# A projection with bias and residual: bias spread by a VectorE shuffle, wider dummy products, early casts on two engines, last store in two column pieces

## Chip, cores, metric

One core of a Trainium2 chip (trn2). The metric is the device time of one execution in microseconds (us). The profile's "span", from its first to its last recorded instruction, is about 1.8 us shorter. Names: PE is TensorE, PEld its weight loads, DVE VectorE, ACT ScalarE, POOL GpSimd, SP SyncE; a "q" behind a name is that engine's instruction queue.

## The reference

```python
batch, m, k, n = 16, 512, 1024, 768          # all fp32
out = np.matmul(x, weight) + bias + residual
```

The 8192 rows are handled as 64 tiles of 128 rows, in eight blocks of eight.

## The kernel before

Per tile: ACT casts x to bf16, PE transposes it (four transposes of paired bf16 words), DVE copies the transposed tile out of PSUM, PE makes 16 products, and DVE adds the result to the residual, to which POOL has already added the bias. The first three tiles go through their products weight quarter by weight quarter, since the weights arrive in quarters. All big loads and stores stand in one list and go through the queue of SP:

```python
HEAD_ORDER = [('bias',), ('warm', 10), ('cast', 0, 'v'), ('cast', 1, 's'), ('tr', 0), ('tr', 1),
 ('wc', 0, 0, 's'), ('wc', 0, 1, 'v'), ('warm', 4), ('mm', 0, 0), ('mm', 1, 0),
 ('cast', 2, 'v'), ('cast', 3, 's'), ('tr', 2), ('tr', 3), ('wc', 1, 0, 's'), ('wc', 1, 1, 'v'),
 # ... cut: the other quarters
 ('cast', 4, 's'), ('mm', 0, 3), ('mm', 1, 3), ('mm', 2, 3)]
ORDER = [('x', 0, 0, 2), ('w', 0, 0, 2), ('x', 0, 2, 4), ('w', 1, 0, 2), ('w', 2, 0, 2), ('w', 3, 0, 2),
 ('x', 0, 4, 6), ('x', 0, 6, 8), ('r', 0, 0, 5), ('x', 1, 0, 4), ('r', 0, 5, 8), ('r', 1, 0, 5),
 ('x', 1, 4, 8), ('x', 2, 0, 8), ('r', 1, 5, 8), ('r', 2, 0, 8), ('x', 3, 0, 8), ('s', 0, 0, 8),
 # ... cut: x, r (residual) and s (store) of the later blocks
 ('s', 4, 0, 8), ('s', 5, 0, 8), ('s', 6, 0, 8), ('s', 7, 0, 5), ('s', 7, 5, 7), ('s', 7, 7, 8)]
```

An entry is (kind, block, first tile, end tile). `'v'` and `'s'` name DVE and ACT, `('warm', n)` is n dummy products that keep PE busy. The bias is one row; a product with a row of ones spreads it over the partitions:

```python
    K_(nc.scalar.dma_start(out=bias_row, in_=bias[None, :]))       # first instruction of ACT's queue
    # ... cut: memsets
    make_identity(nc, ident)
    for _ in range(WARM):                                           # 10
        K_(nc.tensor.matmul(PO[0][:, 0:256], lhsT=warm[:, 0:P], rhs=warm, start=True, stop=True))

    def bias_rows():
        bias_ps = PO[HEAD - 1]
        for n0, nl in chunks:                                       # 512 and 256 columns
            K_(nc.tensor.matmul(bias_ps[:, n0:n0 + nl], lhsT=ones_row,
                                rhs=bias_row[:, n0:n0 + nl], start=True, stop=True))
        K_(nc.vector.tensor_copy(out=bias_sb, in_=bias_ps))
```

The program fixes the order of each engine's instructions (`K_` keeps it), and an instruction that waits holds up the work behind it: below, the cast of tile 0 on DVE stands behind a waiting instruction for 6.2 us.

Of the kernel before, what the change touches and what calls it, by code (L numbers as in the profile page):

```python
# [9 lines left out]
FP32 = mybir.dt.float32  # L10
BF16 = mybir.dt.bfloat16
P = 128
J = 8
X_SLOTS = 2
RO_SLOTS = 4
HEAD = 3
XT_N = 4
XB_N = 4
WARM = 10
EARLY_END = 6  # L20
TMP_SLOT = {0: 3}
ADDS = [6, 0, 7, 8, 1, 9, 2, 10, 3, 11, 4, 12, 5, 13, 14, 15]
HEAD_ORDER = [('bias',), ('warm', 10), ('cast', 0, 'v'), ('cast', 1, 's'), ('tr', 0), ('tr', 1),
 ('wc', 0, 0, 's'), ('wc', 0, 1, 'v'), ('warm', 4), ('mm', 0, 0), ('mm', 1, 0),
 ('cast', 2, 'v'), ('cast', 3, 's'), ('tr', 2), ('tr', 3), ('wc', 1, 0, 's'), ('wc', 1, 1, 'v'),
 ('mm', 2, 0), ('mm', 0, 1), ('mm', 1, 1), ('mm', 2, 1), ('wc', 2, 0, 's'), ('wc', 2, 1, 'v'),
 ('mm', 0, 2), ('mm', 1, 2), ('mm', 2, 2), ('wc', 3, 0, 's'), ('wc', 3, 1, 'v'),
 ('cast', 4, 's'), ('mm', 0, 3), ('mm', 1, 3), ('mm', 2, 3)]
ORDER = [('x', 0, 0, 2), ('w', 0, 0, 2), ('x', 0, 2, 4), ('w', 1, 0, 2), ('w', 2, 0, 2), ('w', 3, 0, 2),
 ('x', 0, 4, 6), ('x', 0, 6, 8), ('r', 0, 0, 5), ('x', 1, 0, 4), ('r', 0, 5, 8), ('r', 1, 0, 5),  # L30
 ('x', 1, 4, 8), ('x', 2, 0, 8), ('r', 1, 5, 8), ('r', 2, 0, 8), ('x', 3, 0, 8), ('s', 0, 0, 8),
 ('r', 3, 0, 8), ('x', 4, 0, 8), ('r', 4, 0, 8), ('s', 1, 0, 8), ('x', 5, 0, 8), ('r', 5, 0, 8),
 ('s', 2, 0, 8), ('x', 6, 0, 8), ('r', 6, 0, 8), ('s', 3, 0, 8), ('x', 7, 0, 8), ('r', 7, 0, 8),
 ('s', 4, 0, 8), ('s', 5, 0, 8), ('s', 6, 0, 8), ('s', 7, 0, 5), ('s', 7, 5, 7),
 ('s', 7, 7, 8)]


@with_exitstack
def kernel(
# [8 lines left out]
    nc = tc.nc  # L48
# [4 lines left out]
    N = weight.shape[1]  # L53
    n_q = K // (2 * P)
    n_t = M // P
    n_s = n_t // J
    chunks = [(0, 512), (512, N - 512)]

    x_d = x2d.rearrange("(S p j) k -> S p j k", p=P, j=J)
    res_d = res2d.rearrange("(S p j) n -> S p j n", p=P, j=J)  # L60
    out_d = out2d.rearrange("(S p j) n -> S p j n", p=P, j=J)
    w_d = weight.rearrange("(q p e) n -> p q e n", p=P, e=2)

    sb = ctx.enter_context(tc.tile_pool(name="sb", bufs=1))
    ps = ctx.enter_context(tc.tile_pool(name="ps", bufs=1, space=bass.MemoryType.PSUM))

    def fixed(pool, name, n, shape, dt):
        return [pool.tile(shape, dt, name=f"{name}", tag=f"{name}{i}", bufs=1) for i in range(n)]

    X = fixed(sb, "x_tile", X_SLOTS, [P, J, K], FP32)  # L70
    R = fixed(sb, "ro", RO_SLOTS, [P, J, N], FP32)
    XB = fixed(sb, "xb", XB_N, [P, K], BF16)
    XT = fixed(sb, "xt", XT_N, [P, n_q, P, 2], BF16)
    PO = fixed(ps, "psum_o", HEAD, [P, N], FP32)
    PT = fixed(ps, "pt", 2, [P, n_q, P], FP32)
    (w_sb,) = fixed(sb, "w_sb", 1, [P, n_q, 2, N], BF16)
    (bias_sb,) = fixed(sb, "bias_sb", 1, [P, N], FP32)
    (bias_row,) = fixed(sb, "bias_row", 1, [1, N], FP32)
    (ones_row,) = fixed(sb, "ones_row", 1, [1, P], FP32)
    (ident,) = fixed(sb, "ident", 1, [P, P], FP32)  # L80
    (warm,) = fixed(sb, "warm", 1, [P, 256], BF16)
    (warm_a,) = fixed(sb, "warm_a", 1, [1, 2], FP32)
    K_ = tc.keep_in_program_order
    w_st = R[1]

    done = set()
    queue = list(ORDER)

    def pump():
        while queue:  # L90
            kind, S, j0, j1 = queue[0]
            if kind == "w":
                need = []
            elif kind == "x":
                need = [("cast", J * (S - X_SLOTS) + j) for j in range(j0, j1)] if S >= X_SLOTS else []
            elif kind == "r":
                need = [("store", S - RO_SLOTS, j) for j in range(j0, j1)] if S >= RO_SLOTS else []
                if S == 1:
                    need = [("wcast", n_q - 1)]
                if S in TMP_SLOT.values():  # L100
                    need = [("add", t) for t in range(EARLY_END) if TMP_SLOT[t // J] == S]
            else:
                need = [("out", J * S + j) for j in range(j0, j1)]
            if not all(n in done for n in need):
                return
            queue.pop(0)
            if kind == "w":
                K_(nc.sync.dma_start(out=w_st[:, 2 * S + j0:2 * S + j1, :], in_=w_d[:, S, j0:j1, :]))
                continue
            if kind == "x":  # L110
                K_(nc.sync.dma_start(out=X[S % X_SLOTS][:, j0:j1, :], in_=x_d[S, :, j0:j1, :]))
            elif kind == "r":
                K_(nc.sync.dma_start(out=R[S % RO_SLOTS][:, j0:j1, :], in_=res_d[S, :, j0:j1, :]))
            else:
                K_(nc.sync.dma_start(out=out_d[S, :, j0:j1, :], in_=R[S % RO_SLOTS][:, j0:j1, :]))
                done.update(("store", S, j) for j in range(j0, j1))
            done.update((kind, J * S + j) for j in range(j0, j1))

    def mark(*what):
        done.add(what)  # L120
        pump()

    def cast(t, how="s"):
        if t < n_t:
            assert ("x", t) in done, t
            src, dst = X[t // J % X_SLOTS][:, t % J, :], XB[t % XB_N]
            if how == "sv":
                K_(nc.scalar.copy(out=dst[:, 0:K // 2], in_=src[:, 0:K // 2]))
                K_(nc.vector.tensor_copy(out=dst[:, K // 2:K], in_=src[:, K // 2:K]))
            else:  # L130
                K_((nc.scalar.copy if how == "s" else nc.vector.tensor_copy)(out=dst, in_=src))  # L131
            mark("cast", t)
# [12 lines left out]
    def mm(t, n0, nl, q, e):  # L145
        K_(nc.tensor.matmul(  # L146
            PO[t % HEAD][:, n0:n0 + nl], lhsT=XT[t % XT_N][:, q, :, e],
            rhs=w_sb[:, q, e, n0:n0 + nl],
            start=(q == 0 and e == 0), stop=(q == n_q - 1 and e == 1),
        ))  # L150

    def row(t, n0=0, nl=N):
        return R[t // J % RO_SLOTS][:, t % J, n0:n0 + nl]

    def tmp(t):
        return R[TMP_SLOT[t // J]][:, t % J, :]
# [17 lines left out]
    def finish(t):  # L174
        p = PO[t % HEAD]
        if t < EARLY_END:
            K_(nc.vector.tensor_add(out=tmp(t), in0=p, in1=bias_sb))  # L177
            mark("fin", t)
        else:
            assert ("add", t) in done, t  # L180
            K_(nc.vector.tensor_add(out=row(t), in0=p, in1=row(t)))  # L181
            mark("out", t)

    K_(nc.scalar.dma_start(out=bias_row, in_=bias[None, :]))
    K_(nc.vector.memset(warm, 0.0))  # L185
    K_(nc.vector.memset(ones_row, 1.0))
    K_(nc.vector.memset(warm_a, 0.0))
    K_(nc.scalar.copy(out=warm_a, in_=warm_a))  # L188
    make_identity(nc, ident)
    for _ in range(WARM):  # L190
        K_(nc.tensor.matmul(PO[0][:, 0:256], lhsT=warm[:, 0:P], rhs=warm, start=True, stop=True))  # L191

    def bias_rows():
        bias_ps = PO[HEAD - 1]
        for n0, nl in chunks:
            K_(nc.tensor.matmul(  # L196
                bias_ps[:, n0:n0 + nl], lhsT=ones_row, rhs=bias_row[:, n0:n0 + nl],
                start=True, stop=True,
            ))
        K_(nc.vector.tensor_copy(out=bias_sb, in_=bias_ps))  # L200

    pump()
    for kind, *a in HEAD_ORDER:
        if kind == "bias":
            bias_rows()
        elif kind == "cast":
            cast(*a)
        elif kind == "warm":
            for _ in range(a[0]):
                K_(nc.tensor.matmul(PO[1][:, 0:256], lhsT=warm[:, 0:P], rhs=warm, start=True, stop=True))  # L210
        elif kind == "tr":
            transp(a[0])
        elif kind == "wc":
            q, e, eng = a
            copy = {"v": nc.vector.tensor_copy, "s": nc.scalar.copy, "g": nc.gpsimd.tensor_copy}[eng]
            K_(copy(out=w_sb[:, q, e, :], in_=w_st[:, 2 * q + e, :]))  # L216
            if (q, e) == (n_q - 1, 1):
                mark("wcast", q)
        else:
            for e in range(2):  # L220
                for n0, nl in chunks:
                    mm(a[0], n0, nl, a[1], e)
    pump()
    for t in range(HEAD - 1):
        finish(t)
        pool_adds(t)

    for t in range(HEAD, n_t):
# [10 lines left out]
    t = n_t - 1  # L239
    tail = [(PO[t % HEAD], 0, 512), (PO[(t - 2) % HEAD], 512, N - 512)]  # L240
    for p, n0, nl in tail:
        for q in range(n_q):
            for e in range(2):
                K_(nc.tensor.matmul(  # L244
                    p[:, 0:nl], lhsT=XT[t % XT_N][:, q, :, e], rhs=w_sb[:, q, e, n0:n0 + nl],
                    start=(q == 0 and e == 0), stop=(q == n_q - 1 and e == 1),
                ))
        K_(nc.vector.tensor_add(out=row(t, n0, nl), in0=p[:, 0:nl], in1=row(t, n0, nl)))  # L248
    mark("out", t)
    pump()  # L250
    assert not queue, queue
# [30 lines left out]
```

## Time and profile before

| what | before | from |
|---|---|---|
| time | 211.45 us median | 4 runs, 211.37 to 211.54 |
| PE busy | 97% of the span | page, part 1 |
| DMA engines, SP's queue | 97.6% of their time | page, part 3 |
| one tile on PE in steady state | 3.036 us | chain in order of time |

These are lines of the page of the kernel before, from its parts 1, 2 and 3. In part 2 each digit is the busy share of one fortieth of the span, in tenths.

```profile
PE 204.3 (97%) x1308; PEld 133.6 (64%) x1308; DVE 104.7 (50%) x139; ACT 68.0 (32%) x68; POOL 114.6 (55%) x70
...
PE   7999999999999999999999999999999999999992
...
DMA  6999999999999999999999999999999999999785
...
q1 hardware_dynamic: 5184, 87.03, 97.6%
```

PE and the DMA engines are both full. PE alone is not the whole story: whatever makes PE earlier needs its data earlier from a queue that has hardly a gap.

The next lines are the timeline of the kernel before in its head. The columns are start, duration, engine, line, operation, what it writes and reads, count, and in brackets the idle time before it with what ended that.

```profile
3.30 2.92 PE L196 MATMUL psum_o<-bias_row,ones_row 1*128 1x512 f32 x4
5.53 1.04 ACT L131 CAST xb<-x_tile 128x1024 bf16<-128x1024 f32 x1 [2.78 <-DMA x_tile<-in_x_dram]
6.26 0.96 DVE L200 COPY bias_sb<-psum_o 128x768 f32<-128x768 f32 x1 [5.12 <-PE psum_o L196]
7.13 0.68 DVE L131 CAST xb<-x_tile 128x1024 bf16<-128x1024 f32 x1
8.26 1.91 PE L139 MATMUL pt<-ident,xb 128*128 128x128 f32 x8
10.82 2.11 PE L146 MATMUL psum_o<-w_sb,xt 128*128 128x512 bf16 x8
14.15 6.75 PE L146 MATMUL psum_o<-w_sb,xt 128*128 128x512 bf16 x40 [0.35 <-DVE xt L140]
```

The bias product starts at 3.30 with no wait for a load, so the bias landed by then. The first x piece lands at 5.53 (ACT's cast), but DVE first copies the bias and casts tile 0 only at 7.13. PE ends its head with 40 products from 14.15 to 20.90.

What the loads leave in slack is read from ACT's casts of tiles 8 to 11 and 12 to 15, in the timeline of ACT alone:

```profile
31.32 3.89 ACT L131 CAST xb<-x_tile 128x1024 bf16<-128x1024 f32 x4 [8.74 <-DMA x_tile<-in_x_dram]
43.61 3.89 ACT L131 CAST xb<-x_tile 128x1024 bf16<-128x1024 f32 x4 [8.41 <-DMA x_tile<-in_x_dram]
```

and from PE's transposes of tiles 8 and 12, in the timeline of PE around 33 and 45 us:

```profile
32.88 0.60 PE L139 MATMUL pt<-ident,xb 128*128 128x128 f32 x4
...
45.03 0.60 PE L139 MATMUL pt<-ident,xb 128*128 128x128 f32 x4
```

Tile 8's cast ends at 31.32 + 1.04 = 32.36, 0.52 us before PE's transpose (0.41 before its first weight load); tile 12's ends at 44.65, 0.38 us before (0.27). A PE more than that ahead would have to wait there.

### The profile page before, as it was taken

To read this page: it belongs to the slowest core of one execution; us is meant where nothing else is said; L and a number is where in the kernel's file an instruction comes from. 1 tells how busy PE (TensorE), PEld (TensorE's weight loads), DVE (VectorE), ACT (ScalarE), POOL (GpSimd) and SP (SyncE) were. 2 spreads that over 40 slices of the span, in tenths; PEclk is the share of its full clock that TensorE was granted. 3 is DMA by queue.
4 is the path that set the end of the run, shared out by engine and by line. 5 is a ranking of instruction groups with operands and counts; after the bars stand their busy time and mean duration, and the time that the engine had idled before them with its cause. 6 is when DMAs were issued, how large, how long until landed. Compare 5 with 4: busy or idle time off the path is not lost.

```text
span 209.6 us, 3135 instructions
## 1 busy us (share of the span) xinstructions
PE 204.3 (97%) x1308; PEld 133.6 (64%) x1308; DVE 104.7 (50%) x139; ACT 68.0 (32%) x68; POOL 114.6 (55%) x70
## 2 busy tenths in 40 slices
PE   7999999999999999999999999999999999999992
PEld 4756666666666666666666666666666666666661
DVE  0473643474375455455544554554455445545542
ACT  2445307060733053323432152330533134321000
POOL 1000099995278980199599702994059910799000
PEclk9999999999999999999999999999999999999999
DMA  6999999999999999999999999999999999999785
GB/s 236 425 434 436 427 403 448 456 406 404 462 450 402 417 441 425 421 458 400 436 458 422 425 403 436 446 441 419 427 427 446 425 413 435 432 419 441 336 379 231
DMA packets 5200, 87.23 MB, mean 416 GB/s; under 512 B 577, under 2 KB 577, under 8 KB 1346
## 3 DMA queue, kind: packets, MB, share of 16 engines
q1 hardware_dynamic: 5184, 87.03, 97.6%
q8 instruction: 10, 0.16, 0.3%
q14 instruction: 4, 0.03, 0.0%
q10 hardware_dynamic: 2, 0.00, 0.0%
HBM read 61.87 MB, written 25.17 MB: 415 GB/s over the span
## 4 chain that ended last, share of the span: by engine, by line
PE 97%; DVE 1%; issue 0%
PE psum_o L146 79%; PE pt L139 14%; PE psum_o L210 1%; PE psum_o L196 1%; PE psum_o L244 1%; PE psum_o L191 1%; DVE xt L140 0%; DVE ro L248 0%; DVE warm L185 0%
## 5 line engine op out<-in xcount | busy, mean ns | idle before, releaser
L146 PE MATMUL psum_o<-w_sb,xt 128*128 128x512 bf16 x1008 | 174.7, 327 | 0.3 <-DVE xt L140 0.3
L146 PEld LDWEIGHTS <-xt 128*128 128x128 bf16 x1008 | 98.8, 98 | 59.1 <-DVE xt L140 0.6
L171 POOL TENSOR_TENSOR ro<-ro,bias_sb 128x768 f32<-128x768 f32 x58 | 103.2, 1818 | 53.5 <-DMA ro<-in_residual_dram 53.5
L131 ACT CAST xb<-x_tile 128x1024 bf16<-128x1024 f32 x62 | 63.2, 1044 | 116.4 <-PE pt L139 58.6
L140 DVE COPY xt<-pt 128x1024 bf16<-128x1024 bf16 x64 | 44.1, 691 | 79.0 <-PE pt L139 78.9
L181 DVE TENSOR_TENSOR ro<-psum_o,ro 128x768 f32<-128x768 f32 x57 | 54.2, 950 | 12.0 <-POOL ro L171 10.9
L139 PE MATMUL pt<-ident,xb 128*128 128x128 f32 x256 | 39.0, 277 | 0.0
L139 PEld LDWEIGHTS pt<-ident,xb 128*128 128x128 f32 x256 | 30.7, 143 | 7.3
L167 POOL TENSOR_TENSOR ro<-ro 128x768 f32<-128x768 f32 x6 | 10.8, 1814 | 25.2 <-DMA ro<-in_residual_dram 25.2
L177 DVE TENSOR_TENSOR ro<-psum_o,bias_sb 128x768 f32<-128x768 f32 x6 | 5.6, 950 | 3.5 <-PE psum_o L146 3.5
L216 ACT CAST w_sb<-ro 128x768 bf16<-128x768 f32 x4 | 3.3, 832 | 3.8 <-DMA ro<-in_weight_dram 3.8
L200 DVE COPY bias_sb<-psum_o 128x768 f32<-128x768 f32 x1 | 1.0, 958 | 5.1 <-PE psum_o L196 5.1
L210 PE MATMUL psum_o<-warm 128*128 128x256 bf16 x14 | 3.4, 416 | 0.0
L191 PE MATMUL psum_o<-warm 128*128 128x256 bf16 x10 | 2.3, 418 | 1.1 <-DVE warm L185 1.1
L196 PE MATMUL psum_o<-bias_row,ones_row 1*128 1x512 f32 (+1 forms) x4 | 2.9, 880 | 0.0
L210 PEld LDWEIGHTS <-warm 128*128 128x128 bf16 x14 | 1.9, 142 | 1.4 <-issue 0.7
L244 PE MATMUL psum_o<-w_sb,xt 128*128 128x512 bf16 (+1 forms) x16 | 2.8, 326 | 0.0
L191 PEld LDWEIGHTS <-warm 128*128 128x128 bf16 x10 | 1.3, 144 | 1.5 <-DVE warm L185 1.1
L244 PEld LDWEIGHTS <-xt 128*128 128x128 bf16 x16 | 1.6, 98 | 1.1
L196 PEld LDWEIGHTS psum_o<-bias_row,ones_row 1*128 1x128 f32 x4 | 1.2, 318 | 1.5 <-issue 1.5
L216 DVE CAST w_sb<-ro 128x768 bf16<-128x768 f32 x4 | 2.0, 553 | 0.0
L188 ACT ACT_TABLE_LOAD x1 | 1.3, 1283 | 1.3 <-PEq L266 1.3
(12 smaller groups left out, 4.0 us busy)
## 6 DMA issues: line engine op xcount, KB each, us to landing
x_tile<-in_x_dram SPq DMA_DIRECT2D x6, 4096.0 KB, 29.8
out_dram<-ro SPq DMA_DIRECT2D x7, 3072.0 KB, 24.7
ro<-in_residual_dram SPq DMA_DIRECT2D x6, 3072.0 KB, 21.3
x_tile<-in_x_dram SPq DMA_DIRECT2D x4, 1024.0 KB, 8.2
x_tile<-in_x_dram SPq DMA_DIRECT2D x2, 2048.0 KB, 25.9
ro<-in_residual_dram SPq DMA_DIRECT2D x2, 1920.0 KB, 22.1
ro<-in_weight_dram SPq DMA_DIRECT2D x4, 768.0 KB, 10.2
ro<-in_residual_dram SPq DMA_DIRECT2D x2, 1152.0 KB, 28.6
```

Of the source, the lines that this page charges most:

```text
L131: K_((nc.scalar.copy if how == "s" else nc.vector.tensor_copy)(out=dst, in_=src))
L139: K_(nc.tensor.transpose(out=pt[:, q, :], in_=words[:, ts(q, P)], identity=ident))
L140: K_(nc.vector.tensor_copy(out=XT[t % XT_N].rearrange("p q m e -> p (q m e)"), in_=pt.rearrange("p q m -> p (q m)").bitcast(BF16),))
L146: K_(nc.tensor.matmul(PO[t % HEAD][:, n0:n0 + nl], lhsT=XT[t % XT_N][:, q, :, e], rhs=w_sb[:, q, e, n0:n0 + nl], start=(q == 0 and e == 0) ...
L167: K_(nc.gpsimd.tensor_add(out=r, in0=r, in1=tmp(t)))
L171: K_(nc.gpsimd.tensor_add(out=r, in0=r, in1=bias_sb))
L177: K_(nc.vector.tensor_add(out=tmp(t), in0=p, in1=bias_sb))
L181: K_(nc.vector.tensor_add(out=row(t), in0=p, in1=row(t)))
L191: K_(nc.tensor.matmul(PO[0][:, 0:256], lhsT=warm[:, 0:P], rhs=warm, start=True, stop=True))
L196: K_(nc.tensor.matmul(bias_ps[:, n0:n0 + nl], lhsT=ones_row, rhs=bias_row[:, n0:n0 + nl], start=True, stop=True,))
L210: K_(nc.tensor.matmul(PO[1][:, 0:256], lhsT=warm[:, 0:P], rhs=warm, start=True, stop=True))
L244: K_(nc.tensor.matmul(p[:, 0:nl], lhsT=XT[t % XT_N][:, q, :, e], rhs=w_sb[:, q, e, n0:n0 + nl], start=(q == 0 and e == 0), stop=(q == n_q ...
```

## The change

Its intent is a shorter head and tail: take the fp32 bias products off PE, warm PE's clock with fewer but wider dummies, get the early x tiles cast sooner, and start the last store in two parts. The bias now goes to partitions 0, 32, 64 and 96 by one load, and a shuffle on DVE copies each of them over its 32 partitions. The shuffle reads the whole tile, so the tile is cleared first.

```diff
-WARM = 10
+WARM = 12
-HEAD_ORDER = [('bias',), ('warm', 10), ('cast', 0, 'v'), ('cast', 1, 's'), ('tr', 0), ('tr', 1),
- ('wc', 0, 0, 's'), ('wc', 0, 1, 'v'), ('warm', 4), ('mm', 0, 0), ('mm', 1, 0),
- ('cast', 2, 'v'), ('cast', 3, 's'), ...
- ('cast', 4, 's'), ...
+HEAD_ORDER = [('bias',), ('cast', 0, 'v'), ('cast', 1, 's'), ('tr', 0), ('tr', 1), ('wc', 0, 0, 's'),
+ ('wc', 0, 1, 'g'), ('mm', 0, 0), ('mm', 1, 0), ('cast', 2, 'sv'), ('cast', 3, 'sv'), ...
+ ('cast', 4, 'sv'), ...
- ('s', 7, 7, 8)]
+ ('c', 7, 7, 0), ('c', 7, 7, 1)]              # last tile: 512 columns, then 256
...
-    K_(nc.scalar.dma_start(out=bias_row, in_=bias[None, :]))
     K_(nc.vector.memset(warm, 0.0))
-    K_(nc.vector.memset(ones_row, 1.0))
+    K_(nc.gpsimd.memset(bias_row, 0.0))                          # 128 x 768
+    K_(nc.scalar.dma_start(
+        out=bias_row.rearrange("(g p) n -> g p n", p=QUAD)[:, 0, :],
+        in_=bias[None, :].to_broadcast([P // QUAD, N]),
+    ))
...
-        K_(nc.tensor.matmul(PO[0][:, 0:256], lhsT=warm[:, 0:P], rhs=warm, start=True, stop=True))
+        K_(nc.tensor.matmul(PO[0][:, 0:512], lhsT=warm[:, 0:P], rhs=warm, start=True, stop=True))
     def bias_rows():
-        ... two products and a copy
+        K_(nc.vector.stream_shuffle(out=bias_sb, in_=bias_row, mask=[0] * QUAD))
```

`'sv'` halves a cast between ACT and DVE; this applies to tiles 2, 3 and 4. `'g'` is a cast on POOL.

## The prediction

> **What bounds the kernel now.** Two resources, both nearly full. The page gives PE 97% of the 209.6 us span; the chain of waits is 97% PE. The main queue's packets take 97.6% of the 16 DMA engines; DMA shows 9 tenths in slices 2 to 37. PE needs 3.036 us a tile (the chain in order of time: transposes 0.44, products 2.60). A tile moves 1.31 MB (x 0.52, residual 0.39, out 0.39), which at the 425 to 432 GB/s of the view by stretches is also about 3.05 us. Loads and stores share one queue and land in order of issue, back to back. So an earlier PE does not make data come earlier.
>
> **The head.** Removed: two fp32 bias products (2.85 us of PE, 3.37 to 6.22; DVE waits for them until 6.26, so cast 0 starts only at 7.13) and 14 dummies. Added: 12 dummies of 512 columns (256 cold columns take 0.21 us, so I estimate 0.43 each, 5.1 in all, ending by 6.3), a POOL memset, and one DVE shuffle of 128x768 fp32. Trainium skill, "VectorE: DVE Perf Modes", perf-mode tier table: the shuffle has only a 1x mode, about 2400 ns for 2048 elements; I estimate 0.9 us for 768; no trace shows it yet. It can run before x lands (5.5), so cast 0 moves to about 5.6-6.0.
>
> The trace shows transposes at 0.21 us each until about 10 us, 0.11 later: PE doubled its speed near 11.9, 5.7 us after the unbroken dummies began. The skill's "TensorE: Matmul & The Clock Gate", Part 1, gives about 3.4 us of sustained work; with dummies unbroken from 1.2 I expect the switch between 4.6 and 8.
>
> Tiles 2 and 3 land at 9.89 either way. Before, DVE cast tile 2 only at 11.28-11.96, behind a weight cast; halved on two engines, both are cast by about 11.1, so products resume near 12.0 instead of 14.15. Weights still land at 11.8, 13.65, 15.5. The head's last product ends near 18.6 instead of 20.9. The split fourth cast sits ahead of the first two finishes on DVE and returns about 0.4.
>
> **How much survives.** Little. Tile 8's x lands at 31.32, its cast ends 32.36, PE loads its first transpose at 32.77: 0.35 us of slack. Tile 12: landing 43.61, cast done 44.65, PE at 44.92: 0.2 us. With landings fixed, PE waits over 1 us at tile 8, a little at tile 12, and runs on only about 0.2 us early. Later x has 3 us or more of slack.
>
> **Tail.** Last product ends 205.7, last add 206.16, last store (384 KB) issued 206.24, landed 2.3 us later. Storing 256 KB at about 205.6 and 128 KB at 206.2 helps, but the 768 KB before it occupies DMA until about 207: I estimate 0.3 us.
>
> **Prediction.** 211.4 - 0.2 - 0.3 = 210.9 us, 210.1 to 211.6. Faster by over 2%: 0.02; within 2%: 0.96; slower: 0.02.
>
> **What would show it.** Head's last product near 19; new PE waits for the casts of tiles 8 and 12 (x landing still near 31.3 and 43.6); then 3.04 us a tile; last product near 205.5; shuffle about 0.9 us; last landing under 2 us after its issue.
>
> **What would make it wrong.** x for tiles 8 and 12 landing earlier (up to 2.5 us more); the wait at tile 8 dropping PE's clock again (1-2 us slower); the POOL weight cast (I estimate 1-1.8 us from POOL's 1.8 us adds) delaying the first products past 10.6; the bias load landing after x, pushing back all DVE work.

## The result, and the profile after

| | before | after |
|---|---|---|
| time, median | 211.45 us (4 runs, 211.37 to 211.54) | 211.92 us (4 runs, 211.76 to 212.4) |
| span profiled | 209.6 us | 210.0 us |
| mean granted clock | 1.0 | 0.992 |

The ratio is 1.0026, with a 95% interval of 1.0008 to 1.0043. A ratio is the mean time of one kernel's fast runs over that of the other's fast runs of the same rounds, so not quite the ratio of the medians. The class, within 2%, was right. The time lies above the range of 210.1 to 211.6, and its sign is opposite to the prediction: 0.5 us slower, not 0.5 us faster. That little changed in total was foreseen, but not for this reason: the head was to become shorter, and it became longer.

The mean granted clock counts the time before the clock's first recorded change as full speed (see the last section), so the two figures cannot be compared for the head: in the kernel before, the starts of equal instructions show half speed until 12.1 us (first 0.21 us from transpose to transpose, then 0.11).

The same lines of the page for the changed kernel:

```profile
PE 201.7 (96%) x1292; PEld 130.5 (62%) x1292; DVE 105.0 (50%) x140; ACT 67.7 (32%) x69; POOL 116.0 (55%) x72
...
PE   7499999999999999999999999999999999999992
...
DMA  6999999999999999999999999999999999999785
...
q1 hardware_dynamic: 5328, 87.03, 97.5%
```

PE works 2.6 us less and the span is longer; the idle time lies in the second slice (5.25 to 10.5 us). Its timeline there:

```profile
1.19 5.23 PE L203 MATMUL psum_o<-warm 128*128 128x512 bf16 x12 [1.19 <-DVE warm_a L199]
...
1.50 1.09 ACTq L195 DMA_DIRECT2D bias_row<-in_bias_dram  x1
...
7.38 1.01 DVE L206 STREAM_SHUFFLE bias_sb<-bias_row 128x768 f32<-128x768 f32 x1
7.84 0.83 ACT L224 CAST w_sb<-ro 128x768 bf16<-128x768 f32 x1 [0.80 <-DMA ro<-in_weight_dram]
7.88 0.82 POOL L224 CAST w_sb<-ro 128x768 bf16<-128x768 f32 x1 [5.90 <-DMA ro<-in_weight_dram]
8.29 0.96 DVE L140 CAST xb<-x_tile 128x1024 bf16<-128x1024 f32 x1
...
9.39 1.73 PE L148 MATMUL pt<-ident,xb 128*128 128x128 f32 x8 [2.97 <-DVE xb L140]
...
11.05 2.44 PE L155 MATMUL psum_o<-w_sb,xt 128*128 128x512 bf16 x8
...
14.71 6.75 PE L155 MATMUL psum_o<-w_sb,xt 128*128 128x512 bf16 x40 [0.35 <-DVE xt L149]
```

The waits of this kernel name the first cause:

```profile
DVE bias_sb L206 <- DMA bias_row<-in_bias_dram: 6.2, 1, 6.2
```

The bias load is issued at 1.50, after POOL's memset, and lands at 7.35. DVE stands still for 6.2 us with the shuffle at its head, and cast 0 behind it starts at 8.29, later than before. PE, done with its dummies at 6.42, idles 2.97 us. Then it is slow: eight transposes take 1.73 us and eight products 2.44 us. The view by stretches shows why (columns: stretch, its length, busy times of PE, PEld, DVE, ACT and POOL, granted clock, DMA share, GB/s):

```profile
6.50:9.00 2.50, 0.00 (x0) 0.00 (x0) 1.64 (x3) 1.38 (x2) 0.82 (x1) 1.00 1.03 436
9.00:9.50 0.50, 0.11 (x1) 0.14 (x2) 0.25 (x1) 0.00 (x0) 0.00 (x0) 1.00 0.93 389
9.50:10.00 0.50, 0.50 (x4) 0.50 (x4) 0.00 (x0) 0.00 (x0) 0.00 (x0) 0.63 0.99 414
10.00:13.00 3.00, 3.00 (x13) 1.66 (x12) 2.05 (x4) 1.90 (x3) 0.00 (x0) 0.50 1.02 426
```

The clock was granted at half speed for 3.4 us, from 9.6 to 13.0. So the change lost again the full speed that its dummies had reached at 6.2 us, well before the 12.1 us of the kernel before. The last product of the head ends at 14.71 + 6.75 = 21.46, 0.56 us after that of before, and the last product of all at 206.25 instead of 205.70: PE waits for nothing in between, so the 0.55 us are kept to the end. The new tail gives a little back: from the last product to the end of the span it is 3.89 us before and 3.79 after.

This profile also shows the first x piece landing at 6.00 instead of 5.53; whether that belongs to the change was to be tested.

### The profile page after: what moved, and what is told of

The parts are those of the page before. It is cut to its first block, busy times and chain, and to the rows that moved or that the text cites. A ratio compares the mean times of both kernels' runs of the same rounds, so it can differ in the third digit from the quotient of the medians.

```text
span 210.0 us, 3110 instructions
## 1 busy us (share of the span) xinstructions
PE 201.7 (96%) x1292; PEld 130.5 (62%) x1292; DVE 105.0 (50%) x140; ACT 67.7 (32%) x69; POOL 116.0 (55%) x72
## 4 chain that ended last, share of the span: by engine, by line
PE 93%; DMA 3%; DVE 1%; issue 1%; POOL 0%; DVEq 0%; POOLq 0%
PE psum_o L155 79%; PE pt L148 14%; DMA bias_row<-in_bias_dram 3%; PE psum_o L253 1%; DVE bias_sb L206 0%; DVE xb L140 0%; DVE xt L149 0%; DVE ro L257 0%; POOL ident masks.py:197 0%; POOL bias_row L194 0%; DVEq L206 0%; POOLq L276 0%
## 5 line engine op out<-in xcount | busy, mean ns | idle before, releaser
L140 ACT CAST xb<-x_tile 128x1024 bf16<-128x1024 f32 x60 | 61.2, 1044 | 112.7 <-PE pt L148 60.9
L190 DVE TENSOR_TENSOR ro<-psum_o,ro 128x768 f32<-128x768 f32 x57 | 54.2, 950 | 11.7 <-POOL ro L180 10.5
L203 PE MATMUL psum_o<-warm 128*128 128x512 bf16 x12 | 5.2, 626 | 1.2 <-DVE warm_a L199 1.2
L203 PEld LDWEIGHTS <-warm 128*128 128x128 bf16 x12 | 1.7, 145 | 3.9 <-issue 2.7
L224 POOL CAST w_sb<-ro 128x768 bf16<-128x768 f32 x1 | 0.8, 822 | 5.9 <-DMA ro<-in_weight_dram 5.9
L137 ACT CAST xb<-x_tile 128x512 bf16<-128x512 f32 x3 | 1.8, 617 | 3.4 <-DMA x_tile<-in_x_dram 3.4
L138 DVE CAST xb<-x_tile 128x512 bf16<-128x512 f32 x3 | 1.2, 422 | 1.9 <-DMA x_tile<-in_x_dram 1.9
L257 DVE TENSOR_TENSOR ro<-psum_o,ro 128x512 f32<-128x512 f32 (+1 forms) x2 | 1.1, 558 | 0.9 <-PE psum_o L253 0.8
L224 DVE CAST w_sb<-ro 128x768 bf16<-128x768 f32 x3 | 1.5, 554 | 0.0
```

The costliest lines, as they stand in the source:

```text
L137: K_(nc.scalar.copy(out=dst[:, 0:K // 2], in_=src[:, 0:K // 2]))
L140: K_((nc.scalar.copy if how == "s" else nc.vector.tensor_copy)(out=dst, in_=src))
L190: K_(nc.vector.tensor_add(out=row(t), in0=p, in1=row(t)))
L203: K_(nc.tensor.matmul(PO[0][:, 0:512], lhsT=warm[:, 0:P], rhs=warm, start=True, stop=True))
L224: K_(copy(out=w_sb[:, q, e, :], in_=w_st[:, 2 * q + e, :]))
```

## The experiments

Theory: the late bias load blocks DVE (wait), PE idles and loses its clock (slow clock), and the gains of the head cannot reach the end because x for tiles 8 and 12 lands when it lands (pinning). Rivals: it is not the shuffle's place but something else in the change; it is the four-row form of the load, not its lateness; the wait matters and the clock does not; nothing pins PE. Each run was timed in five rounds against the kernel before on the same chip, which gave four to six times of its own kernel and 9 or 11 of the kernel before.

| run | median us | before, same chip | ratio (95% interval) |
|---|---|---|---|
| late_shuffle | 211.40 | 211.52 | 0.9999 (0.9986 to 1.0011) |
| tail_only | 211.28 | 211.52 | 0.999 (0.9978 to 1.0003) |
| before_late_bias | 213.71 | 211.52 | 1.0105 (1.009 to 1.0121) |
| before_four_rows | 213.37 | 211.52 | 1.0096 (1.0081 to 1.0112) |
| after_again | 211.94 | 211.35 | 1.0029 (1.0012 to 1.0045) |
| filled_gap | 211.37 | 211.35 | 1.0003 (0.9991 to 1.0015) |
| loads_moved | 211.09 | 211.35 | 0.999 (0.9977 to 1.0003) |
| before_loads_moved | 211.41 | 211.35 | 0.9998 (0.9986 to 1.001) |
| loads_moved_fine | 211.54 | 211.58 | 1.0002 (0.9984 to 1.0019) |
| late_shuffle_fine | 211.77 | 211.58 | 1.0003 (0.9987 to 1.0019) |

All ten gave correct results.

### late_shuffle: the shuffle no longer first on DVE

```diff
-HEAD_ORDER = [('bias',), ('cast', 0, 'v'), ...
+HEAD_ORDER = [('cast', 0, 'v'), ...
- ('wc', 3, 0, 's'), ('wc', 3, 1, 'v'), ('cast', 4, 'sv'), ...
+ ('wc', 3, 0, 's'), ('wc', 3, 1, 'v'), ('bias',), ('cast', 4, 'sv'), ...
```

> The changed kernel with one move: the bias shuffle stands behind the third weight casts in VectorE's order instead of first. Theory (the shuffle, waiting until 7.35 us for the bias load, blocked cast 0, left TensorE idle 3 us and let its clock fall): cast 0 starts at about 6.0 us, the first transpose before 7.2 us, no stretch at clock 0.5 longer than 1 us, the head's last product before 20 us instead of 21.5. Whether that reaches the time: if x for tiles 8 and 12 still lands near 31.9 and 44.2 us, TensorE waits there and the time is 211.5 to 211.8 us (0.1 to 0.4 below the changed kernel). Rival (landings do not pin TensorE): the time falls by the full 1.5 to 2.2 us, to about 210. Rival (the loss has nothing to do with the shuffle's place): 211.9 us again.

Its timeline on PE:

```profile
6.43 1.42 PE L148 MATMUL pt<-ident,xb 128*128 128x128 f32 x8
8.33 1.46 PE L155 MATMUL psum_o<-w_sb,xt 128*128 128x512 bf16 x8 [0.49 <-ACT w_sb L224]
10.61 1.18 PE L148 MATMUL pt<-ident,xb 128*128 128x128 f32 x8 [0.82 <-ACT xb L137]
12.05 6.75 PE L155 MATMUL psum_o<-w_sb,xt 128*128 128x512 bf16 x39 [0.26 <-DVE xt L149]
...
32.81 0.66 PE L148 MATMUL pt<-ident,xb 128*128 128x128 f32 x4 [1.45 <-ACT xb L140]
...
45.06 0.66 PE L148 MATMUL pt<-ident,xb 128*128 128x128 f32 x4
```

and on ACT around tiles 8 and 12:

```profile
31.71 3.89 ACT L140 CAST xb<-x_tile 128x1024 bf16<-128x1024 f32 x4 [9.09 <-DMA x_tile<-in_x_dram]
43.96 3.89 ACT L140 CAST xb<-x_tile 128x1024 bf16<-128x1024 f32 x4 [8.36 <-DMA x_tile<-in_x_dram]
```

The head now does what the prediction said of it: products resume at 12.05 and end at 18.80, 2.1 us earlier than before. Then PE waits 1.45 us for the cast of tile 8. It transposes tile 12 at 45.06, when before did at 45.03. The cast of tile 12 ends at 43.96 + 1.04 = 45.00, so PE could not have come earlier. The 2.1 us are gone, and the time is that of before. So the place of the shuffle did cause the loss, and the landings do pin. The time, 211.40, came out just below what was expected (211.5 to 211.8).

### tail_only: the column split alone, on the kernel before

```diff
- ('s', 7, 7, 8)]
+ ('c', 7, 7, 0), ('c', 7, 7, 1)]
```

> The kernel before with only the last tile's store cut in two column pieces. My prediction says 0.3 us faster (211.15); the comparison of the two profiles says 0.1 to 0.15 (from the last product's end to the end of the span 3.9 us before, about 3.75 after). Rival: the short rows of the second piece cost as much as the overlap wins, 0.0.

Measured: 0.24 us in the medians, ratio 0.999 with an interval that includes 1. The estimate of 0.3 us is compatible with this, and so is half of it; the times cannot say which. Its profile shows 0.08 us: from the last product to the end of the span it is 3.81 us instead of 3.89.

### before_late_bias and before_four_rows: late issue or broadcast form

Late: the kernel before, its one-row load placed behind a memset of the same size.

```diff
-    K_(nc.scalar.dma_start(out=bias_row, in_=bias[None, :]))
     K_(nc.vector.memset(warm, 0.0))
+    K_(nc.gpsimd.memset(bias_full, 0.0))                  # 128 x 768; bias_row is its row 0
+    K_(nc.scalar.dma_start(out=bias_row, in_=bias[None, :]))
```

> The kernel before, its one-row bias load put behind a GpSimd memset of a 128x768 tile as in the change (issue near 1.5 us instead of 0.7). Theory (a load issued after the x and weight loads have filled the DMA engines lands late, whatever its form): it lands at 5.5 to 7.5 us, TensorE's bias products start there instead of at 3.3, and the time rises by 2 to 4 us, to 213.5 to 215.5. Rival (the broadcast form of four rows is what is slow): it lands by 4 us and the time stays within 0.5 us of 211.45. First x piece lands at 5.5 us if the form of the load delayed x, at 6.0 if the time of its issue did.

Form: the kernel before, its load issued first but to four partitions.

```diff
-    K_(nc.scalar.dma_start(out=bias_row, in_=bias[None, :]))
+    K_(nc.scalar.dma_start(out=bias_full.rearrange("(g p) n -> g p n", p=32)[:, 0, :],
+                           in_=bias[None, :].to_broadcast([4, N])))
```

> The kernel before, its bias load in the four-row broadcast form of the change, but issued first as before and with no memset; the products read row 0 only. Theory (lateness, not form): lands by about 3.5 us, TensorE's bias products start within 0.3 us of 3.3, time 211.4 to 211.7. Rival (form): landing after 5 us and a time above 213. The first x piece lands at 6.0 instead of 5.5 us if the form of the load is what delayed x by 0.46 us, at 5.5 if not.

The bias product of before_late_bias, in its timeline (3.30 in before):

```profile
6.45 2.89 PE L198 MATMUL psum_o<-bias_row,ones_row 1*128 1x512 f32 x4 [3.08 <-DMA bias_row<-in_bias_dram]
```

The issue and the bias product of before_four_rows:

```profile
0.73 1.08 ACTq L185 DMA_DIRECT2D bias_row<-in_bias_dram  x1
...
5.66 2.90 PE L200 MATMUL psum_o<-bias_row,ones_row 1*128 1x512 f32 x4 [2.29 <-DMA bias_row<-in_bias_dram]
```

I had set lateness against form as rivals, and that was wrong: either one suffices. The late one-row load landed 4.9 us after its issue (1.50 to 6.4). The early four-row load also took 4.9 us (0.73 to 5.6). A likely reason is that its issue takes 1.08 us instead of 0.50 and so ends only at 1.81, when the x load issued at 0.74 was already moving (from 1.74); no run changes the issue time alone. Each costs about 2 us of time here, since PE itself waits for the bias. The first x piece landed at 5.55 and 5.62 us: neither delays x.

The Trainium skill, "DMA: Bandwidth & Descriptors", section "Queues, rings and completion order", says that each DMA engine takes turns between queues only at packet boundaries, where a packet is typically about 9 to 17 descriptors. In the profile of the kernel before, SP's queue has 5184 records (the page calls them packets) for 36 loads and stores on 16 engines, 9 each, so an engine's whole share of one could be a single turn. An estimate from that and the trace: the first x piece is 1024 KB, 64 KB for each of 16 engines, or 2.4 us at the 430 GB/s measured; the first weight piece 768 KB, 1.8 us. A small load that comes after them could wait one or two such turns, 2 to 4 us, which fits the 4.9 to 5.9 us seen.

The packed traces also hold the times of single DMA records, which no view of the profile prints. They show the wait itself. A row of the bias takes 0.12 to 0.20 us to move. In before it moved at 1.63 to 1.83 us, ahead of the first record of x (1.75). The four early rows of before_four_rows moved at 4.77 to 4.97, just after the first DMA engine had finished its share of the first x piece (4.67). The late row of before_late_bias moved at 5.62, when that piece was done (5.18), and the rows of the changed kernel between 5.49 and 6.69. So the bytes were not slow, they stood in line. Which engine a record ran on is not recorded, so the turns of one engine are not shown.

### after_again: the changed kernel once more

> The changed kernel unaltered. Open so far: in its profile the first x piece landed at 6.00 us, in five other profiles (before, the three with other bias loads, late_shuffle) at 5.50 to 5.62. If that was chance of one execution: 5.5 to 5.6 here, and the bias load lands near 6.5 to 7. If it belongs to the changed kernel: 6.0 again. Either way theory says the time stays 0.3 to 0.6 us above before, since TensorE's resumption is timed by the shuffle and not by x: head's last product 21.2 to 21.5 us.

The time repeats: 211.94 us, ratio 1.0029. The first x piece landed at 5.44 us, so the 6.00 was chance of one execution. The shuffle again came at 7.25. In this execution PE idled 3.42 us, from 5.58 to 9.00, the clock stood at 0.50 from 7.9 to 14.8 us, and the head's last product ended at 22.05, outside the 21.2 to 21.5 expected. So the loss varies with how long the clock stays low; the six runs spread from 211.43 to 212.62, those of before on that chip from 211.22 to 211.65. All ten timed executions of the changed kernel bear this out: the seven with a mean granted clock of 0.991 or 0.992, as in the first profile, took 211.43 to 212.14 us, the three with 0.980 or 0.981, as in the second, 212.40 to 212.62.

### filled_gap: the wait without the slow clock

```diff
-HEAD_ORDER = [('bias',), ('cast', 0, 'v'), ('cast', 1, 's'), ('tr', 0), ...
+HEAD_ORDER = [('bias',), ('cast', 0, 'v'), ('cast', 1, 's'), ('warm', 14), ('tr', 0), ...
```

> The changed kernel with 14 more dummies of 512 columns ahead of the first transposes, to keep TensorE busy while the shuffle waits for the bias load. It parts the two halves of the head's loss: the wait and the slow clock after it. Theory: the clock stays at 1.0 through 9 to 13 us (0.5 in the changed kernel), the eight first transposes take about 1.0 us instead of 1.73 and the eight first products 1.3 instead of 2.44; the head's last product comes about 1 to 1.3 us earlier, near 20.2; the time falls only to that of late_shuffle, 211.3 to 211.7, because x of tiles 8 and 12 then holds TensorE. If the clock was not what cost the second half: head's last product stays at 21.3 to 21.5 and the time at 211.9.

In its timeline on PE the first transposes are only 0.36 us earlier than in the changed kernel (9.39), but quick:

```profile
9.03 1.06 PE L148 MATMUL pt<-ident,xb 128*128 128x128 f32 x8 [0.77 <-DVE xb L140]
10.44 1.47 PE L155 MATMUL psum_o<-w_sb,xt 128*128 128x512 bf16 x8 [0.35 <-DVE xt L149]
...
13.14 6.75 PE L155 MATMUL psum_o<-w_sb,xt 128*128 128x512 bf16 x40 [0.35 <-DVE xt L149]
```

and its stretch from 10 to 13 us, to be held against the 0.50 above:

```profile
10.00:13.00 3.00, 2.44 (x17) 1.58 (x16) 2.26 (x5) 1.90 (x3) 0.00 (x0) 1.00 1.02 426
```

The shuffle still waits until 7.24 and cast 0 starts at 8.20. Yet the head ends at 19.89, 1.57 us earlier than in the changed kernel, and the time is 211.37 us against 211.94 on the same chip, equal to before. (Single times of the two overlap, 211.27 to 211.80 against 211.43 to 212.62; their ratios to before, 1.0003 and 1.0029, have intervals that barely touch, and the first measurement of the changed kernel gave 1.0026 as well. The mean granted clock was 0.998 or more in all five runs.) So the wait by itself would have been harmless: what it left of the head was still 1.0 us ahead of before, more than the pin lets through, as PE's wait for the cast of tile 8 shows:

```profile
PE pt L148 <- ACT xb L140: 0.6, 1, 0.6
```

The slow clock that came after the idle stretch pushed the head past the point where the pin hides it.

### loads_moved and before_loads_moved: the pin taken away

The residual of tiles 0 to 4, which is needed late, goes behind the second x block, and POOL adds in the matching order.

```diff
- ('r', 0, 0, 5), ('x', 1, 0, 4), ('r', 0, 5, 8), ('r', 1, 0, 5), ('x', 1, 4, 8), ('x', 2, 0, 8), ('r', 1, 5, 8), ...
+ ('x', 1, 0, 4), ('r', 0, 5, 8), ('r', 1, 0, 5), ('x', 1, 4, 8), ('r', 0, 0, 5), ('x', 2, 0, 4), ('r', 1, 5, 8), ('x', 2, 4, 8), ...
-ADDS = [6, 0, 7, 8, 1, 9, 2, 10, 3, 11, 4, 12, 5, 13, 14, 15]
+ADDS = [6, 7, 8, 9, 10, 11, 12, 0, 1, 2, 3, 13, 4, 14, 5, 15]
```

loads_moved does this on late_shuffle, the control before_loads_moved on the kernel before. (POOL's list is also made to keep strictly to this order.)

> late_shuffle with the order of the early loads changed: the residual of tiles 0 to 4, which nothing needs soon, behind the second x block; GpSimd's adds in the matching order (6 to 12 first). If landings pin TensorE (my reading: late_shuffle gains 2 us in the head and loses them all at tiles 8 and 12), x of tile 8 lands near 26.5 and that of tile 12 near 38 us, the waits go, and the gain stays to the end: last product near 203.8, time 209.2 to 209.9. If something else holds TensorE later, or the DMA queue as a whole is the limit, the time stays at 211 to 211.5.

> The control: the kernel before with the same reordering of loads and adds. TensorE waits for no landing there, so by the pinning theory nothing is gained: 211.3 to 211.7. If the reordering is good in itself (or harms by itself), this run moves as much as loads_moved does against late_shuffle.

The control does not move (211.41 against 211.35). In loads_moved the pin is gone: ACT finds tile 8 at 26.77 and tile 12 at 39.05 us, the waits for tiles 8 and 12 vanish, and PE's last product ends at 203.8, 1.9 us earlier than before.

```profile
26.77 3.89 ACT L140 CAST xb<-x_tile 128x1024 bf16<-128x1024 f32 x4 [4.35 <-DMA x_tile<-in_x_dram]
```

But the time is 211.09, not 209.2 to 209.9. The end of its span in the view by stretches:

```profile
202.00:204.00 2.00, 1.81 (x13) 0.99 (x11) 1.12 (x3) 0.00 (x0) 0.00 (x0) 1.00 0.91 382
204.00:206.00 2.00, 0.00 (x0) 0.00 (x0) 0.27 (x1) 0.00 (x0) 0.00 (x0) 1.00 0.96 379
206.00:208.00 2.00, 0.00 (x0) 0.00 (x0) 0.00 (x0) 0.00 (x0) 0.00 (x0) 0.84 0.24 89
```

PE is done at 203.8 and the DMA engines work on: all 16 to 206.0, then ever fewer, until 208.1. The single DMA records show it: from 207.0 to 207.9 about two are under way at a time, as two engines would give, and the last ends at 208.06. In before all 16 engines end their last store within 0.16 us (208.07 to 208.23). So a second wall stands behind the first. It is less the amount of data, as the rival had it, than its uneven end: at 206.2 only 133 KB are left, by an estimate 0.3 us at 430 GB/s, but they take 1.9 us on so few engines. No run evens this out, so what an even finish would gain is not shown. The Trainium skill, "DMA: Bandwidth & Descriptors", section "Latency and other measured facts", says that two of the 16 DMA engines (7 and 15) are usually slower than the others in traces, but as a best guess puts it down to loads issued by GpSimd, and there are none here; no view here names the late engines either, so their cause stays open.

### loads_moved_fine and late_shuffle_fine: smaller last stores

```diff
- ('s', 6, 0, 8), ('s', 7, 0, 5), ('s', 7, 5, 7), ('c', 7, 7, 0), ('c', 7, 7, 1)]
+ ('s', 6, 0, 4), ('s', 6, 4, 8), ('s', 7, 0, 2), ('s', 7, 2, 4), ('s', 7, 4, 5), ('s', 7, 5, 6), ('s', 7, 6, 7), ('c', 7, 7, 0), ('c', 7, 7, 1)]
```

> loads_moved with the last two blocks stored in smaller pieces (4+4 tiles, then 2, 2, 1, 1, 1, 2/3, 1/3 tile). In loads_moved the last product ended 1.9 us earlier than before, but the span only 0.3 us: data then drained to 206.3 us on most DMA engines and to 208.2 on two or three of the 16, after slices at 0.84 to 0.91 busy (192-194, 196-198, 200-204 us) in which a store waited for its last tile. If those gaps are the wall, filling them gains 0.5 to 0.8 us: 210.3 to 210.6. If the queue's total work or the few late engines are the wall, 210.9 to 211.2 as loads_moved.

> The same finer stores on late_shuffle, where TensorE still ends near 205.8 us. The last third of a tile then waits behind 384 KB less data. Theory: the tail is set by the backlog in front of the last piece (data until 208.1 in late_shuffle, last product 205.8), so 0.4 to 0.7 us are gained, 210.7 to 211.0. If the fixed time from issue to landing sets it, 211.3 to 211.5.

Neither gained (ratios 1.0002 and 1.0003), and I had expected 0.4 to 0.8 us. loads_moved_fine has fewer gaps (0.97 to 1.03 busy from 192 to 202 us), but its data still drains to 207.9, again with about two records under way at the end (0.12 of the capacity from 207 to 208); so it is in late_shuffle_fine, until 208.5. Gaps between stores were not the wall; what stands at the end is the few late engines.

No version beats both kernels by a clear margin. The best, loads_moved, is 0.26 us under before with an interval that includes 1.

## Why the prediction was wrong, point by point

- **Two full resources; an earlier PE does not make data earlier.** Right. late_shuffle showed the first consequence (2.1 us lost at tiles 8 and 12), loads_moved the second (1.9 us gained on PE, of which 0.3 us were left at the end of the span, since the last stores drained late).
- **The shuffle about 0.9 us.** 1.01 us, and 1.03 in a second execution. The skill's 2400 ns for 2048 elements, scaled, is close.
- **"It can run before x lands (5.5), so cast 0 moves to about 5.6-6.0."** This is the step that failed. The shuffle ran at 7.38 and cast 0 at 8.29. I took for granted that the bias would be there as early as before, without costing its load: issued at 1.50 behind the memset, in a form whose issue takes 1.09 us, and so behind the first x load. It landed at 7.35, 5.9 us after its issue. Each of the two alone gives 4.9 us, where the early one-row load had needed at most 2.6. I had named "the bias load landing after x" as a risk, but put no time on it and left it out of the sum.
- **The clock rises between 4.6 and 8.** It did in the first profile of the changed kernel, at 6.2 us by the clock records of the packed trace. But this was partly luck: with the same unbroken dummies from 1.2 us it rose at 4.5 in the second profile, at 3.8 in filled_gap and at 7.2 in late_shuffle, where the starts of the dummies and transposes come closer at those times. And I looked for a fall only at tile 8. It fell at 9.6, after the idle stretch that the late bias made; with the clock kept up in filled_gap, the 0.57 us between 211.94 and 211.37 are gone. At tile 8 the wait of 1.45 us in late_shuffle brought no fall.
- **Products resume near 12.0, the head ends near 18.6, little of it survives.** Right, once the bias does not block: 12.05 and 18.80 in late_shuffle. Of the 0.2 us that I let survive nothing did; x of tiles 8 and 12 landed 0.39 and 0.35 us later there (31.71, 43.96).
- **The tail, 0.3 us.** 0.24 in the medians of tail_only, not told apart from none; 0.08 by its profile and 0.10 by that of the changed kernel.
- **POOL's weight cast, 1 to 1.8 us, as a risk.** 0.82 us, and harmless.

In the sum 211.4 - 0.2 - 0.3 the term of the head was wrong in sign: the last product came 0.55 us later instead of 0.2 earlier.

## What to carry to other kernels

When a load is changed, follow it to its landing: a few kilobytes issued one microsecond later, or as four rows instead of one, can come out behind megabytes and land many microseconds later, and the first instruction that needs it then blocks its whole engine. Put an instruction that waits for such a load behind work that does not need it. An idle stretch early in a kernel can cost less than the slow clock that follows it, so keep dummy products running until real work is sure to be ready; and before counting a gain in the head, read the slack of the next landings, and behind that how long the last DMA engines need to drain.

## What the Trainium skill lacked or had wrong

- "TensorE: Matmul & The Clock Gate", Part 1, has the clock fall after at least one idle window of about 3.4 us. The trace agrees with the length (half speed for 3.4 us in the changed kernel, 6.8 in its second profile), but the window need not be wholly idle. In the first profile the clock rose at 6.2 and fell at 9.6 us, and PE worked 0.4 us of the 3.4 between (to 6.42 and from 9.39). In the second it rose at 4.5 and fell at 7.9, with 1.1 us of work between (to 5.58). 1.45 us of idleness at tile 8 of late_shuffle did not make it fall. The page gives no busy share for a fall.
- "DMA: Bandwidth & Descriptors", "Latency and other measured facts", ties its two slow DMA engines, as a best guess, to loads issued by GpSimd. Here all big transfers are issued by SP, and yet about two of the 16 engines drained 1.9 us longer than most (206.2 to 208.1 us in loads_moved). Whether they are the same two is not known.
- "TensorE: Matmul & The Clock Gate", Part 1, warns that recorded clock events can be unreliable, but not that the granted clock in the views used here reads 1.00 until the clock's first recorded change, whatever the clock is. In the kernel before it is 1.00 from 6 to 12 us, while transposes take 0.21 us each until about 10 us and 0.11 us in the steady state. The spacing of equal instructions is the safer sign.
- "DMA: Bandwidth & Descriptors", "Queues, rings and completion order", tells how engines take turns between queues, but gives no figure for a small load behind large ones: 4.9 us for 3 KB, 4.9 and 5.9 us for 12 KB here, at most 2.6 us when a 3 KB load went first.
- No page that I found gives the time that a queue needs to issue a load by its form: here 1.08 us for four broadcast rows against 0.50 for one row, on ACT's queue, and 0.38 to 0.43 us for the first loads to 128 partitions on SP's.
